# Paired strips of a two-layer decoder: the fourth block summed in the third sum's bank, and the down strips' block sums made of turned tiles

## The chip, the cores and the metric

The kernel runs on one core of one Trainium2 chip. The metric is the time of one execution on the device in microseconds (us); the time before is the median of three runs. A profile is one further execution, taken with the hardware profiler. Its engines are PE (TensorE, matmul), PEld (its weight loads), DVE (VectorE), ACT (ScalarE), POOL (GpSimd) and SP (SyncE, which here only issues DMAs).

## The reference

Two layers of a decoder work on x, 256 rows of 2048 in fp32. Each layer has a mixer (window attention and a gated linear recurrence, side by side, joined by a matrix `w_out`), a gated FFN of width 5632 and a gated addition of per-layer inputs (called ple below):

```
h = rms_norm(x, pre_mix_gain[i])
m = concat([attention, recurrence]) @ w_out[i]
x = x + rms_norm(m, post_mix_gain[i])
h = rms_norm(x, pre_ffn_gain[i])
f = (silu(h @ w_ffn_gate[i]) * (h @ w_ffn_up[i])) @ w_ffn_down[i]
x = x + rms_norm(f, post_ffn_gain[i])
gate = sigmoid(rms_norm(x, ple_gain[i]) @ w_ple_gate[i])
x = x + (p[i] @ w_ple_proj[i]) * gate
```

## The kernel before

**Products.** Every matrix product is made in three matmuls, since each fp32 operand is kept as a high and a low part: high by high, low by high, high by low. Weights come in pieces of 256 x 512 (`wr`, 128 partitions x 1024), fetched by SP's queue. ACT makes the high part by a cast (`wh`, L305), DVE the low part by a subtraction (`wl`, L315). There are ten buffers of `wr` and seven each of `wh` and `wl`, so a cast can run only some pieces ahead of PE. Activations stand turned, with the contraction on the partitions, as high and low parts in tiles `ck`. An output strip is 512 columns wide and has two row halves (t = 0, 1) of 128 rows, each with a bank of PSUM; matmuls have the shape 128 x 128 times 128 x 512. There are two pools of PSUM banks, four banks each: "acc" (`psum(...)`) and "ms" (`bank()`). Temporary tiles of 128 x 512 come from the pool `nat`, twelve buffers.

**A pair of strips.** `paired` (L399) makes two strips at once from the same left side: wa's strip with the banks e (`acce`, half 0) and a (`acca`, half 1), and wb's with c (`accc`) and d (`accd`). For two contraction pieces of 256 (three with `half`), it needs seven block products in place of eight: sums of blocks of the left side (`mixed` L360, `mixed_half`) and differences of weight blocks (`sub`, L434 on DVE) are multiplied, and the results are added. `fast()` does that part. A bank u of the pool "ms" runs through three sums: the first is copied by ACT (`saved`, L427) to x[0]; `second()` goes on in the same bank and copies it to y[0]; `third()` goes on again and copies it to x[1]. p5, the copy of a first sum in c, gets u added on DVE (L496) and becomes y[1]. All other pieces follow in `plain`, a loop over pieces that feeds two banks. d is a fresh bank, taken after all this, with the plain products alone. At the end `done_a` and `done_b` take a bank and the saved sum that belongs to it, and add them on DVE (`summed`, L395, or the down strips' `done`, L1229).

`paired` runs 20 times in each layer: twice for `w_out`; ten times for a gate strip with its up strip (`gated`, n = 1 to 10); seven times for the down strips; once for the ple gate (`after` given).

**Groups of the FFN.** Hidden strips come in groups of 2, 3, 3 and 3 (`FF_GROUPS`). `gated(n)` makes hidden strip n: gate by silu on ACT (L1184), times up on DVE (L1191), a transpose in 32 x 32 blocks on DVE (L251), a store and a fetch by DMA that put the blocks in their places (`shuffled`; the fetched tile is called d there), and then, some ticks later (`later`; a tick is a step of the loop over pieces), a split into a high part by ACT (L203) and a low part by DVE (L204): the `ck` tiles of that strip. When a group is complete, its four down strips follow: strips 0 and 1 as a pair, then 2 and 3 as a pair (in the last group these two go singly). The block sums for these pairs are made by `mixed(first)`, eight ticks after the last gated strip starts, of the `ck` tiles of the group's first hidden strip: two full adds of high and low (L367), four sums of quarters (L373), and two splits. In groups of three, the first down pair has `mixed_order`: the plain products of both strips but the last two pieces, with `second` inside, and then the last two pieces, since the group's last hidden strip is just being split. (The build takes group 0 with three gated strips, 0 to 2, ahead of its down strips of 0 and 1.)

**Order.** The code gives a program order. The framework's scheduler lays the instructions of each engine into a queue at build time, moving products between the places where the data permit it; each engine runs its queue in order, and waits are semaphores. The names with numbers in the rows of the order are tiles (`wl_6236`), and a bank of "ms" is `ms_...`, whichever of u or others it holds.

Of the kernel before, what the change touches and what calls it, by code (L numbers as in the profile page):

```python
# [9 lines left out]
F32R = mybir.dt.float32r  # L10
# [5 lines left out]
P = 128  # L16
# [31 lines left out]
def decoder(ctx: ExitStack, tc: tile.TileContext, x, p, positions, w_in, attn_sinks,  # L48
# [328 lines left out]

    def mixed_half(x):
# [20 lines left out]
    def paired(lhs, sums, wa, wb, cols, done_a, done_b, nch=8, row0=0, skews=(0, 0),  # L399
               after=None, mixed_order=False, half=None):  # L400
# [41 lines left out]
        def fast():  # L442
            mix = sums()
            r11, r12 = fetch_w(wa, base, cols[0]), fetch_w(wb, base, cols[1])
            if half:
                more = half()
                g, p = fetch_w(wa, base + 2, cols[0]), fetch_w(wb, base + 2, cols[1])
            r21, r22 = fetch_w(wa, base + 1, cols[0]), fetch_w(wb, base + 1, cols[1])
            u = bank()
            acc(u, block(0, 0), parts(r11))  # L450
            if half:
                gx = parts(g)
                acc(u, block(2, 0), gx, (0,))
# [10 lines left out]
            acc(e, block(1, 0), parts(r21))  # L464
            if half:
                acc(e, block(2, 0), gx, (1,))
# [3 lines left out]
            acc(a, block(1, 1), parts(r21))  # L470
            if half:
# [3 lines left out]
                acc(a, block(2, 1), g24, (1,))  # L475
# [11 lines left out]
            def third():  # L487
# [8 lines left out]
                V.tensor_tensor(p5, u, p5, op=ALU.add)  # L496
                y.append(p5)
                tick()
            return e, a, c, x, y, second, third

        head = 3 if half else 2

        def plain(w, col, banks, skew, end, c0=head, c1=nch, then=None):
            n = c1 - c0
            ws = {}
            for i in range(n + skew):
                if i < n:
                    ws[i] = load_w(w, base + c0 + i, col)
                    acc(banks[0], block(c0 + i, 0), ws[i])
                    if i == n - 1 and end:  # L510
                        end(0)
                if i >= skew:
                    acc(banks[1], block(c0 + i - skew, 1), ws[i - skew])
# [6 lines left out]
        e, a, c, x1, x2, second, third = fast()  # L520
# [23 lines left out]
        d = psum("accd")  # L544
# [205 lines left out]
    for l in range(DEPTH):  # L750
# [427 lines left out]
        def gated(n, last, first):  # L1178
            col = n * W
            gate = {}  # L1180

# [8 lines left out]
            def done_up(t, ps):  # L1190
                V.scalar_tensor_tensor(gate[t], ps, rx2(t)[:, 0:1], gate[t],  # L1191
                                       op0=ALU.mult, op1=ALU.mult)
                d = shuffled(gate[t], slow=False)
                later(wait, lambda: split_shuffled(d, None, hl, t))

# [7 lines left out]
            if last:  # L1203
# [131 lines left out]
```

## Time and profile before

| | |
|---|---|
| median of three runs | 2377.96 us |
| lowest, highest | 2377.86, 2381.11 us |
| the profiled execution | 2380.66 us |
| its span | 2378.9 us |
| granted TensorE clock, mean | 0.998 |
| HBM read, written | 474.57 MB, 29.36 MB |

A row of a group reads: line, engine, operation, output <- inputs, shape, count | busy us, mean ns of one | idle time of the engine just before them and what ended most of it. A row of the timeline reads: start, duration, engine, line, operation, count and, in brackets, the idle time before it with what ended it. A row of the waits: who waited for what, us in total, times, longest. A row of the windows: from:to, length, busy time (and count) of PE, PEld, DVE, ACT and POOL, then PE's granted clock, DMA's share and GB/s. A matmul's own duration (0.39) is longer than its distance to the next, since they are pipelined.

### The profile page before, as it was taken

Reading aid. Unit: us, or ns where it says so; the run is one execution under the profiler, and the core shown is the slowest. Engines: PE = TensorE matmul, PEld = TensorE weight load, DVE = VectorE, ACT = ScalarE, POOL = GpSimd, SP = SyncE. Lnnn points to the kernel's source line nnn. Section 1 sums busy time; section 2 is a strip of 40 time slices with the busy share of each in tenths; the row PEclk is TensorE's granted clock in tenths of the full one; section 3 lists DMA queues with packets and bytes.
Section 4 is the critical chain, followed back from the end, with each engine's and each line's share of the span. In section 5 each row is a group of like instructions: output and inputs, shape, how many; then the busy total and the mean of one; then the engine's idle time right before and its main releaser. Section 6 shows DMA issues by size and latency. Waiting matters only on the chain.

```text
span 2378.9 us, 31721 instructions
## 1 busy us (share of the span) xinstructions
PE 2358.3 (99%) x10951; PEld 1950.6 (82%) x10951; DVE 2026.5 (85%) x2703; ACT 1398.0 (59%) x2000; POOL 106.6 (4%) x213
## 2 busy tenths in 40 slices
PE   9999999999999999999999999999999999999999
PEld 7888887887888888888788888878878888888887
DVE  7687987999999899888777879779999989998885
ACT  6565466556556555657556554665566565565564
POOL 3100001000000000001010000010000000000010
PEclk9999999999999999999999999999999999999999
DMA  8666467657566664766776663675765575667753
GB/s 290 216 187 203 151 199 250 223 199 244 181 226 219 241 230 166 272 220 203 227 222 207 184 209 132 226 257 180 241 219 193 206 254 198 230 209 251 243 169 133
DMA packets 301666, 506.05 MB, mean 213 GB/s; under 512 B 23712, under 2 KB 69696, under 8 KB 301504
## 3 DMA queue, kind: packets, MB, share of 16 engines
q1 hardware_dynamic: 301200, 503.93, 63.6%
q8 instruction: 86, 1.41, 0.2%
q14 instruction: 76, 0.62, 0.1%
q10 hardware_dynamic: 240, 0.07, 0.0%
q0 software_dynamic: 64, 0.02, 0.0%
HBM read 474.57 MB, written 29.36 MB: 212 GB/s over the span
## 4 chain that ended last, share of the span: by engine, by line
PE 92%; DVE 4%; issue 1%; DMA 1%; ACT 1%; POOL 1%; SPq 0%; DVEq 0%; ACTq 0%; POOLq 0%
PE acc L331 9%; PE acc L330 9%; PE acc L333 9%; PE accc L418 5%; PE accc L421 5%; PE accc L422 5%; PE acca L422 4%; PE acce L422 4%; PE acce L418 4%; PE acca L418 4%; PE acca L421 4%; PE acce L421 4%; PE accd L422 3%; PE accd L418 3%; PE accd L421 3%; PE ms L418 3%
## 5 line engine op out<-in xcount | busy, mean ns | idle before, releaser
L305 ACT CAST wh<-wr 128x1024 fp32r<-128x1024 f32 x980 | 1006.0, 1051 | 722.9 <-DVE wr L434 209.3
L315 DVE TENSOR_TENSOR wl<-wr,wh 128x1024 fp32r<-128x1024 f32 x980 | 1163.0, 1217 | 212.7 <-ACT wh L305 204.9
L330 PE MATMUL acc<-wh,ck 128*128 128x512 f32 x1056 | 417.5, 396 | 0.8 <-ACT ck L203 0.8
L331 PE MATMUL acc<-wh,ck 128*128 128x512 f32 x1056 | 413.4, 392 | 0.0
L333 PE MATMUL acc<-wl,ck 128*128 128x512 f32 x1056 | 412.2, 391 | 0.8 <-DVE wl L315 0.8
L434 DVE TENSOR_TENSOR wr<-wr 128x1024 f32<-128x1024 f32 (+1 forms) x240 | 243.8, 1038 | 0.8
L333 PEld LDWEIGHTS acc<-wl,ck 128*128 128x128 f32 x1056 | 198.7, 188 | 43.0 <-DVE wl L315 1.7
L331 PEld LDWEIGHTS acc<-wh,ck 128*128 128x128 f32 x1056 | 198.9, 188 | 40.3 <-DVE ck L204 0.4
L330 PEld LDWEIGHTS acc<-wh,ck 128*128 128x128 f32 x1056 | 198.5, 188 | 40.6 <-ACT ck L203 1.0
L418 PE MATMUL acca<-wh,ck 128*128 128x512 f32 x468 | 182.6, 390 | 3.1 <-ACT wh L305 3.1
L422 PE MATMUL acca<-wl,ck 128*128 128x512 f32 x468 | 182.3, 390 | 1.1 <-DVE wl L315 1.1
L418 PE MATMUL acce<-wh,ck 128*128 128x512 f32 x468 | 182.7, 390 | 0.4 <-ACT wh L305 0.4
L422 PE MATMUL acce<-wl,ck 128*128 128x512 f32 x468 | 182.3, 390 | 0.3 <-DVE wl L315 0.2
L421 PE MATMUL acce<-wh,ck 128*128 128x512 f32 x468 | 182.1, 389 | 0.0
L421 PE MATMUL acca<-wh,ck 128*128 128x512 f32 x468 | 182.1, 389 | 0.0
L422 PE MATMUL accd<-wl,ck 128*128 128x512 f32 x368 | 144.7, 393 | 0.0
L418 PE MATMUL accd<-wh,ck 128*128 128x512 f32 x368 | 143.7, 390 | 0.0
L421 PE MATMUL accd<-wh,ck 128*128 128x512 f32 x368 | 143.2, 389 | 0.0
L421 PE MATMUL accc<-wh,ck 128*128 128x512 f32 x368 | 143.2, 389 | 0.0
L422 PE MATMUL accc<-wl,ck 128*128 128x512 f32 x368 | 143.2, 389 | 0.0
L418 PE MATMUL accc<-wh,ck 128*128 128x512 f32 x368 | 143.1, 389 | 0.0
L418 PEld LDWEIGHTS acca<-wh,ck 128*128 128x128 f32 x468 | 87.8, 188 | 22.9 <-ACT wh L305 4.8
(277 smaller groups left out, 3362.2 us busy)
## 6 DMA issues: line engine op xcount, KB each, us to landing
wr<-in_w_in_dram SPq DMA_DIRECT2D x176, 512.0 KB, 4.9
wr<-in_w_ffn_gate_dram SPq DMA_DIRECT2D x176, 512.0 KB, 6.0
wr<-in_w_ffn_up_dram SPq DMA_DIRECT2D x176, 512.0 KB, 6.1
wr<-in_w_ffn_down_dram SPq DMA_DIRECT2D x176, 512.0 KB, 7.4
wr<-in_w_out_dram SPq DMA_DIRECT2D x64, 512.0 KB, 4.9
wr<-in_w_ple_gate_dram SPq DMA_DIRECT2D x64, 512.0 KB, 5.5
turn<-nat SPq DMA_DIRECT2D x86, 256.0 KB, 2.6
nat<-turn SPq DMA_DIRECT2D x344, 64.0 KB, 3.6
```

Source lines behind the costliest of these rows:

```text
L305: marks["hi"] = S.copy(hi, raw)
L315: marks["lo"] = V.tensor_tensor(lo, raw, hi.bitcast(F32), op=ALU.subtract)
L330: T.matmul(ps[t], xh, hi[:, k], start=first, stop=False)
L331: T.matmul(ps[t], xl, hi[:, k], start=False, stop=False)
L333: marks[t, c] = marks["pe"] = T.matmul(ps[t], xh, lo[:, k], start=False, stop=last)
L418: T.matmul(ps, xh, hi[:, k], start=id(ps) not in opened, stop=False, skip_group_check=True)
L421: T.matmul(ps, xl, hi[:, k], start=False, stop=False, skip_group_check=True)
L422: marks["pe"] = T.matmul(ps, xh, lo[:, k], start=False, stop=k == ks[-1], skip_group_check=True)
L434: V.tensor_tensor(dst, p, q, op=ALU.subtract)
```

## The change

Two things are changed.

First, the bank d is no longer a fresh one: u, once `third()` has copied it to x[1], simply takes the plain products of the fourth block on top of its sum. So the add of u to p5 (L496) is gone, and `done_b(1)` adds the bank and p5 as they are. In `paired` with `after` (ple), u is taken from the pool "acc" as `accu`; elsewhere it stays in "ms", now until the end of the pair. In the rows of the order the fourth block's products are therefore those on u's `ms_...`.

Second, the down strips' block sums are made by `mixed_turned`, of the two fetched tiles d of the group's second hidden strip (both row halves), before they are split, and no longer of the `ck` tiles of the first. The two full adds (L367) fall away there, the four sums of quarters are made on other views. It runs two ticks after that strip's split was set for. The pair's sums then stand for the second hidden strip (`q=2`: pieces 2 and 3), so these weight pieces are fetched first, and the plain products run over pieces 0, 1, 4, 5 (`rest`).

```diff
+    def mixed_turned(d):
+        out = [[nat((P, 2, 2, P), F32R) for i in range(2)] for _ in range(2)]
+        a = [[x[0][:, 2 * c:2 * c + 2] for x in d] for c in range(2)]
+        s = [nat((P, 2, 2, P)) for _ in range(2)]
+        s1, s2, s3, s4 = (quarters(s[i][:, j]) for i in range(2) for j in range(2))
+        for dst, p, q, op in ((s1, a[0][1], a[1][1], ALU.add), (s2, s1, a[0][0], ALU.subtract),
+                              (s3, a[0][0], a[0][1], ALU.subtract), (s4, a[1][0], s2, ALU.subtract)):
+            V.tensor_tensor(dst, p, q, op=op)
+        for i in range(2):
+            split(s[i], out[0][i], out[1][i])
+        return lambda i: lambda k: tuple(a[(i - 1) // 2][:, (i - 1) % 2, k] for a in out)
...
-            u = bank()
-            acc(u, block(0, 0), parts(r11))
+            u = psum("accu") if after else bank()
+            acc(u, block(q, 0), parts(r11))
...
                 x.append(saved(u))
-                V.tensor_tensor(p5, u, p5, op=ALU.add)
                 y.append(p5)
...
-        e, a, c, x1, x2, second, third = fast()
+        e, a, c, d, x1, x2, second, third = fast()
...
-            plain(wa, cols[0], (e, a), 0, None, c1=nch - 2, then=second)
+            plain(wa, cols[0], (e, a), 0, None, cs=rest[:-2], then=second)
             third()
-            d = psum("accd")
-            plain(wb, cols[1], (c, d), 0, None, c1=nch - 2)
-            plain(wa, cols[0], (e, a), 0, end_a, c0=nch - 2)
-            plain(wb, cols[1], (c, d), 0, end_b, c0=nch - 2)
+            plain(wb, cols[1], (c, d), 0, None, cs=rest[:-2])
+            plain(wa, cols[0], (e, a), 0, end_a, cs=rest[-2:])
+            plain(wb, cols[1], (c, d), 0, end_b, cs=rest[-2:])
...
-        d = psum("accd")
         plain(wb, cols[1], (c, d), skews[1], end_b)
...
                 d = shuffled(gate[t], slow=False)
+                turned.append(d)
                 later(wait, lambda: split_shuffled(d, None, hl, t))
+                if quad and t == 1:
+                    later(wait + 2, lambda: hx.append(mixed_turned(turned)))
...
-            if last:
-                later(8, lambda: hx.append(mixed(first)))
...
-                           mixed_order=s == 1 and glen > 2)
+                           mixed_order=s == 1 and glen > 2, q=2)
```

In the changed file the lines stand 9 to 14 further down: L305, L315, L203, L204 and L251 are as before; the products of `acc` are L431, L434 and L435 (before L418, L421, L422), `saved` is L440, `sub` L447, `summed` L408, the up strip's product L1202.

The order on PE, at the mixed-order pair of the second group of layer 0. Before, from the last products of acca on a plain piece (`acca_6126` ends just ahead of these rows) to the first product of the second sum (`ms_6086` is u, `accd_6213` is d):

```order
L418 MATMUL accd_6213<-wh_6216,ck_5354 128x512 [waits Activation_49]
L421 MATMUL accd_6213<-wh_6216,ck_5355 128x512
L418 MATMUL acce_6113<-wh_6252,ck_5705 128x512 [waits Activation_49]
L422 MATMUL accd_6213<-wl_6218,ck_5354 128x512 [waits DVE_49]
L418 MATMUL accd_6213<-wh_6216,ck_5354 128x512
L421 MATMUL accd_6213<-wh_6216,ck_5355 128x512
L422 MATMUL accd_6213<-wl_6218,ck_5354 128x512
L418 MATMUL accd_6213<-wh_6234,ck_5354 128x512
L421 MATMUL accd_6213<-wh_6234,ck_5355 128x512
L421 MATMUL acce_6113<-wh_6252,ck_5706 128x512 [waits DVE_49]
L422 MATMUL accd_6213<-wl_6236,ck_5354 128x512 [waits DVE_49]
L418 MATMUL ms_6086<-wh_6158,nat_5944 128x512 [waits Activation_49]
```

The same place now (`ms_6062` is u):

```order
L431 MATMUL acca_6102<-wh_6150,ck_4623 128x512
L434 MATMUL acca_6102<-wh_6150,ck_4624 128x512
L435 MATMUL acca_6102<-wl_6152,ck_4623 128x512
L431 MATMUL acce_6089<-wh_6226,ck_5687 128x512 [waits Activation_49]
L434 MATMUL acce_6089<-wh_6226,ck_5688 128x512 [waits DVE_49]
L431 MATMUL ms_6062<-wh_6134,nat_5925 128x512 [waits Activation_49]
```

The nine products of d have moved away from between acca and the second sum; the two products of acce on the newly split hidden strip (`ck_5687` its high part by ACT, `ck_5688` its low part by DVE) are left.

DVE at the same place, from a product of gate and up to the low part of that hidden strip (`ck_5706` before, `ck_5688` now). Before:

```order
L1191 SCALAR_TENSOR_TENSOR nat_5903<-nat_5830,ry0_4017,nat_5903 128x512 [waits DVE_49]
L1191 SCALAR_TENSOR_TENSOR nat_5963<-nat_5759,ry1_4070,nat_5963 128x512 [waits DVE_49]
L251 STREAM_TRANSPOSE nat_6052<-nat_5903 128x4x4x32 [waits DVE_49]
L315 TENSOR_TENSOR wl_6129<-wr_6082,wh_6127 128x1024 [waits Activation_49]
L315 TENSOR_TENSOR wl_6144<-wr_6140,wh_6142 128x1024 [waits DMAHW2_49,Activation_49]
L315 TENSOR_TENSOR wl_6160<-wr_6078,wh_6158 128x1024 [waits Activation_49]
L251 STREAM_TRANSPOSE nat_6069<-nat_5963 128x4x4x32 [waits DVE_49]
L315 TENSOR_TENSOR wl_6176<-wr_6172,wh_6174 128x1024 [waits DMAHW3_49,Activation_49]
L315 TENSOR_TENSOR wl_6192<-wr_6084,wh_6190 128x1024 [waits PE_49,Activation_49]
L315 TENSOR_TENSOR wl_6202<-wr_6080,wh_6200 128x1024 [waits PE_49,Activation_49]
L315 TENSOR_TENSOR wl_6218<-wr_6214,wh_6216 128x1024 [waits DMAHW4_49,PE_49,Activation_49]
L204 TENSOR_TENSOR ck_5706<-nat_6056,ck_5705 128x4x128 [waits DMAHW4_49,DMAHW3_49,DMAHW5_49,DMAHW2_49,Activation_49]
```

Now:

```order
L251 STREAM_TRANSPOSE nat_6028<-nat_5885 128x4x4x32 [waits DVE_49]
L1202 SCALAR_TENSOR_TENSOR nat_5940<-nat_5741,ry1_4066,nat_5940 128x512 [waits DVE_49]
L315 TENSOR_TENSOR wl_6120<-wr_6116,wh_6118 128x1024 [waits DMAHW2_49,Activation_49]
L315 TENSOR_TENSOR wl_6136<-wr_6054,wh_6134 128x1024 [waits Activation_49]
L315 TENSOR_TENSOR wl_6152<-wr_6148,wh_6150 128x1024 [waits DMAHW3_49,Activation_49]
L251 STREAM_TRANSPOSE nat_6045<-nat_5940 128x4x4x32 [waits DVE_49]
L315 TENSOR_TENSOR wl_6168<-wr_6060,wh_6166 128x1024 [waits PE_49,Activation_49]
L315 TENSOR_TENSOR wl_6178<-wr_6056,wh_6176 128x1024 [waits PE_49,Activation_49]
L315 TENSOR_TENSOR wl_6192<-wr_6188,wh_6190 128x1024 [waits DMAHW4_49,PE_49,Activation_49]
L315 TENSOR_TENSOR wl_6210<-wr_6206,wh_6208 128x1024 [waits DMAHW5_49,PE_49,Activation_49]
L315 TENSOR_TENSOR wl_6228<-wr_6224,wh_6226 128x1024 [waits DMAHW6_49,PE_49,Activation_49]
L204 TENSOR_TENSOR ck_5688<-nat_6032,ck_5687 128x4x128 [waits DMAHW5_49,DMAHW4_49,DMAHW6_49,DMAHW3_49,Activation_49]
```

Ahead of these rows stand, before, the two adds of L395; now the add of accc, one wl, the first product of gate and up, and the other add. From the add of accc to the low part there are thus seven wl before and nine now, and the rest is the same. On ACT the two instructions ahead of the second sum have changed places: the cast of one more weight piece (`wh_6244`) now stands ahead of the cast of `ck_5687`.

PE at the first down pair of group 0, which has no mixed order. Before (`accd_5141` is d, `ms_5190` the next pair's u, `ms_5012` this pair's u):

```order
L418 MATMUL accd_5141<-wh_5144,ck_4274 128x512 [waits Activation_49]
L421 MATMUL accd_5141<-wh_5144,ck_4275 128x512
L418 MATMUL ms_5190<-wh_5191,ck_3826 128x512 [waits Activation_49]
L422 MATMUL accd_5141<-wl_5146,ck_4274 128x512 [waits DVE_49]
L418 MATMUL accd_5141<-wh_5144,ck_4274 128x512
L421 MATMUL accd_5141<-wh_5144,ck_4275 128x512
L422 MATMUL accd_5141<-wl_5146,ck_4274 128x512
L418 MATMUL accd_5141<-wh_5162,ck_4274 128x512
L421 MATMUL accd_5141<-wh_5162,ck_4275 128x512
L421 MATMUL ms_5190<-wh_5191,ck_3827 128x512
L422 MATMUL accd_5141<-wl_5164,ck_4274 128x512 [waits DVE_49]
L418 MATMUL ms_5012<-wh_5084,nat_4868 128x512 [waits Activation_49]
```

Now (`ms_5176` is the next pair's u, `ms_5000` this pair's):

```order
L435 MATMUL acca_5040<-wl_5090,ck_3822 128x512
L431 MATMUL ms_5176<-wh_5177,ck_4270 128x512 [waits Activation_49]
L434 MATMUL ms_5176<-wh_5177,ck_4271 128x512
L435 MATMUL ms_5176<-wl_5179,ck_4270 128x512 [waits DVE_49]
L431 MATMUL ms_5000<-wh_5072,nat_4861 128x512 [waits Activation_49]
```

The nine products of d are gone from here too; three of the next pair's first sum stand ahead of the second sum, one more than before, the third on a low part (`wl_5179`) that DVE makes after two other pieces and a split.

More of the change, by code (lines that the diff above doesn't have):

```diff
@@ L399, in paired @@
     def paired(lhs, sums, wa, wb, cols, done_a, done_b, nch=8, row0=0, skews=(0, 0),
-               after=None, mixed_order=False, half=None):
+               after=None, mixed_order=False, half=None, q=0):
         base = row0 // (2 * P)
@@ L443, in fast @@
             mix = sums()
-            r11, r12 = fetch_w(wa, base, cols[0]), fetch_w(wb, base, cols[1])
+            r11, r12 = fetch_w(wa, base + q, cols[0]), fetch_w(wb, base + q, cols[1])
             if half:
                 more = half()
-                g, p = fetch_w(wa, base + 2, cols[0]), fetch_w(wb, base + 2, cols[1])
-            r21, r22 = fetch_w(wa, base + 1, cols[0]), fetch_w(wb, base + 1, cols[1])
-            u = bank()
-            acc(u, block(0, 0), parts(r11))
+                g, p = fetch_w(wa, base + q + 2, cols[0]), fetch_w(wb, base + q + 2, cols[1])
+            r21, r22 = fetch_w(wa, base + q + 1, cols[0]), fetch_w(wb, base + q + 1, cols[1])
+            u = psum("accu") if after else bank()
+            acc(u, block(q, 0), parts(r11))
             if half:
                 gx = parts(g)
-                acc(u, block(2, 0), gx, (0,))
+                acc(u, block(q + 2, 0), gx, (0,))
             x = [saved(u)]
@@ L463, in fast @@
             e = psum("acce")
-            acc(e, block(1, 0), parts(r21))
+            acc(e, block(q + 1, 0), parts(r21))
             if half:
-                acc(e, block(2, 0), gx, (1,))
+                acc(e, block(q + 2, 0), gx, (1,))
             sub(r11, r22, r11)
@@ L469, in fast @@
             a = psum("acca")
-            acc(a, block(1, 1), parts(r21))
+            acc(a, block(q + 1, 1), parts(r21))
             if half:
@@ L474, in fast @@
                 g24 = parts(g)
-                acc(a, block(2, 1), g24, (1,))
+                acc(a, block(q + 2, 1), g24, (1,))
                 sub(p[:, 0], p[:, 1], p[:, 0])
@@ L495, in third, with plain @@
                 x.append(saved(u))
-                V.tensor_tensor(p5, u, p5, op=ALU.add)
                 y.append(p5)
                 tick()
[L499 to L504, printed above, removed]
+            return e, a, c, u, x, y, second, third
+        rest = [i for i in range(nch) if not q <= i < q + (3 if half else 2)]
+        def plain(w, col, banks, skew, end, cs=rest, then=None):
+            n = len(cs)
             ws = {}
@@ L507, in plain @@
                 if i < n:
-                    ws[i] = load_w(w, base + c0 + i, col)
-                    acc(banks[0], block(c0 + i, 0), ws[i])
+                    ws[i] = load_w(w, base + cs[i], col)
+                    acc(banks[0], block(cs[i], 0), ws[i])
                     if i == n - 1 and end:
@@ L512, in plain @@
                 if i >= skew:
-                    acc(banks[1], block(c0 + i - skew, 1), ws[i - skew])
+                    acc(banks[1], block(cs[i - skew], 1), ws[i - skew])
                 if then and i == 0:
@@ L1176, in decoder, with gated @@
         sx = []
-        def gated(n, last, first):
+        def gated(n, last, quad):
             col = n * W
             gate = {}
+            turned = []
             def done_gate(t, ps):
@@ L1213, in decoder @@
                 n = len(hidden)
-                gated(n, n == want - 1, hidden[ff0] if n > ff0 else None)
+                gated(n, n == want - 1, n == want - 2)
             hid = hidden[ff0:ff0 + glen]
```

## The prediction

> **What bounds the kernel now.** I read the page's first part, then the groups by line, the waits of PE, and then the timeline at the places where the order of instructions changes. First the busy times:
>
> ```profile
> PE 2358.3 (99%) x10951; PEld 1950.6 (82%) x10951; DVE 2026.5 (85%) x2703; ACT 1398.0 (59%) x2000; POOL 106.6 (4%) x213
> ```
>
> PE is busy for 2358.3 of 2378.9 us, so there are about 20 us in which it does nothing, and the change leaves its number of products alone. What the change can win is therefore some of those 20 us; what it can lose has no such limit. The groups that the change removes, whole or in part, are DVE's:
>
> ```profile
> L496 DVE TENSOR_TENSOR nat<-ms,nat 128x512 f32<-128x512 f32 x40 | 27.4, 684 | 3.7 <-ACT nat L427 3.7
> L367 DVE TENSOR_TENSOR nat<-ck 128x512 f32<-128x512 f32 x28 | 18.7, 681 | 0.0
> ```
>
> and the waits of PE that could go with them are few:
>
> ```profile
> PE acca L418 <- ACT wh L305: 3.1, 4, 1.3
> PE ms L418 <- ACT nat L427: 2.2, 1, 2.2
> ```
>
> So the question is at each pair of strips: which product is next on PE's queue, and is its operand there?
>
> **Part 1, DVE's work.** 40 adds of L496 go (27.4 us), and 16 of the 28 of L367 (16 x 0.681 = 10.9 us): the eight groups of down strips lose two each. DVE falls from 2026.5 to about 1988 us, 84% of the span. DVE as a whole bounds nothing at 85%, so of these 38 us I count only what shows at a named place. The four quarter sums stay, the turned tiles live two ticks longer, and the weight pieces come in another order but in the same number on SP's queue; nothing in PE's list of waits names a tile of nat or a fetch at a down pair, so I take 0, at most 1 us in all if one add (0.68) is late once or twice.
>
> **Part 2, the fourth block waits for a copy.** The fourth block's first product now writes the bank that ACT has just to copy. In a gated pair:
>
> ```profile
> 467.08 0.58 ACT L427 COPY nat<-ms 128x512 f32<-128x512 f32 x1
> ...
> 468.14 0.39 PE L418 MATMUL accd<-wh,ck 128*128 128x512 f32 x1
> ```
>
> The copy ends at 467.08 + 0.58 = 467.66, 0.48 before the product that must now wait for it, behind six products of accc that stay between. So at the 20 gated pairs the wait is hidden; without that cover it would cost up to 6 x 0.227 = 1.4 each. At the first pair of w_out the copy is later:
>
> ```profile
> 332.09 0.58 ACT L427 COPY nat<-ms 128x512 f32<-128x512 f32 x1
> ...
> 332.47 0.39 PE L418 MATMUL accd<-wh,ck 128*128 128x512 f32 x1
> ```
>
> 332.67 is 0.20 too late for 332.47, but one or two more products stand in between in the new order (0.23 each): 0.05, at most 0.25, at two places: **+0.1**.
>
> **Part 3, the fillers ahead of the second sum.** This is the largest term. Before, the fourth block had a bank of its own, and nine of its products stood between the last product of acca and the second sum (the first rows of the order, in the section on the change). They cannot stand there any more: the bank's three sums must be made and copied first. At the mixed-order pairs only two products of acce are left in between, and the second of these needs the low part of the turned hidden strip (ck, L204) from DVE. PE before, from the end of accc of the strip ahead to the second sum:
>
> ```profile
> 648.16 0.39 PE L422 MATMUL accc<-wl,ck 128*128 128x512 f32 x1
> ...
> 660.40 0.39 PE L422 MATMUL acca<-wl,ck 128*128 128x512 f32 x1
> 660.63 0.39 PE L418 MATMUL accd<-wh,ck 128*128 128x512 f32 x1
> ...
> 662.78 0.40 PE L421 MATMUL acce<-wh,ck 128*128 128x512 f32 x1
> ...
> 663.35 0.39 PE L418 MATMUL ms<-wh,nat 128*128 128x512 f32 x1
> ```
>
> One product starts 0.227 after another when nothing is waited for (660.40 to 660.63). DVE in the same time:
>
> ```profile
> 649.48 0.68 DVE L395 TENSOR_TENSOR nat<-accc,nat 128x512 f32<-128x512 f32 x1
> 650.08 0.68 DVE L395 TENSOR_TENSOR nat<-accd,nat 128x512 f32<-128x512 f32 x1
> 650.68 1.41 DVE L1191 SCALAR_TENSOR_TENSOR nat<-nat,ry 128x512 f32<-128x512 f32 x2
> 652.00 0.70 DVE L251 STREAM_TRANSPOSE nat<-nat 128x512 f32<-128x512 f32 x1
> 652.63 3.46 DVE L315 TENSOR_TENSOR wl<-wr,wh 128x1024 fp32r<-128x1024 f32 x3
> 656.00 0.70 DVE L251 STREAM_TRANSPOSE nat<-nat 128x512 f32<-128x512 f32 x1
> 656.63 4.59 DVE L315 TENSOR_TENSOR wl<-wr,wh 128x1024 fp32r<-128x1024 f32 x4
> 661.13 0.68 DVE L204 TENSOR_TENSOR ck<-nat,ck 128x512 fp32r<-128x512 f32 x1
> ```
>
> There is no idle time in this stretch: from the add of accc to the end of L204 at 661.81, DVE does two adds, two L1191, two transposes, seven wl and the split. In the new order it does the same and two more wl (nine), each 1.14 apart ((656.00 - 652.63)/3 = 1.12, (661.13 - 656.63)/4 = 1.13, so 2.27 for two). The add of accc can't start before accc's last product has ended, 648.16 + 0.39 = 648.55, some 648.60 with the signal: a head start of 0.88. The three adds that go just ahead of this stretch (two of L367, one of L496, about 2.0 us) are enough for that, so I take it whole. The split then ends at 661.81 + 2.27 - 0.88 = 663.20, and at 664.08 without a head start. Product 2 of acce starts at 663.25, and the second sum 0.23 after that, 663.48, where PE with nothing to wait for would be at 660.40 + 3 x 0.227 = 661.08. Lost 2.40. The old rows lost 663.35 - (660.40 + 12 x 0.227 = 663.12) = 0.23 by small waits. Net 2.17 at each of six places (two further groups in this layer, three in the next): **+13.0**. The bound from below: were DVE in time, ACT would still be late:
>
> ```profile
> 659.10 0.62 ACT L203 CAST ck<-nat 128x512 fp32r<-128x512 f32 x1 [0.16 <-DMA nat<-turn]
> 660.60 1.06 ACT L305 CAST wh<-wr 128x1024 fp32r<-128x1024 f32 x1 [0.89 <-PE acca L421]
> 661.56 0.58 ACT L427 COPY nat<-ms 128x512 f32<-128x512 f32 x1
> ```
>
> On ACT the cast of a weight piece that waits for PE until 660.60 now stands ahead of the cast of ck: 661.56, then 0.62 to 662.18, product 1 at 662.23 where it stood free at 660.63. 1.6 less 0.23 is 1.4 each, 8.2 in all. From above: 3.05 each (no head start), 18.3. The order shows these rows at six places; their times I read at this one.
>
> **Part 4, group 0.** Its first down pair has no mixed order. The new order puts three products of the next pair's first sum between acca and the second sum, and the third needs a wl:
>
> ```profile
> 532.52 0.39 PE L422 MATMUL acca<-wl,ck 128*128 128x512 f32 x1
> ...
> 535.45 0.39 PE L418 MATMUL ms<-wh,nat 128*128 128x512 f32 x1
> ...
> 546.36 0.39 PE L422 MATMUL acce<-wl,ck 128*128 128x512 f32 x1
> 548.04 0.50 PE L418 MATMUL acca<-wh,ck 128*128 128x512 f32 x1 [1.30 <-ACT wh L305]
> 548.38 0.40 PE L421 MATMUL acca<-wh,ck 128*128 128x512 f32 x1
> 549.00 0.50 PE L418 MATMUL acce<-wh,ck 128*128 128x512 f32 x1 [0.22 <-ACT wh L305]
> ```
>
> ```profile
> 533.85 2.35 DVE L315 TENSOR_TENSOR wl<-wr,wh 128x1024 fp32r<-128x1024 f32 x2
> ```
>
> Up to that wl DVE does the same set of instructions as before up to the end of this row, 536.20, less a head start taken as in part 3: 535.32, and the product 0.05 later. It would be due at 532.52 + 3 x 0.227 = 533.20, so 2.17 lost; the old rows lost 535.45 - 532.52 - 12 x 0.227 = 0.2. Against that the waits at 546.36 go, since DVE's four subtractions for the next weights now stand ahead of the last adds and L496 is gone: (1.68 - 0.23) + (0.62 - 0.23) and two starts of 0.11 = 2.06. Net -0.1 at two places: **-0.2** (from -4.1, if wl is in time, to +1.6 without the head start). The end of group 0's second pair:
>
> ```profile
> 570.88 0.39 PE L422 MATMUL acce<-wl,ck 128*128 128x512 f32 x1
> 571.52 0.50 PE L418 MATMUL acca<-wh,ck 128*128 128x512 f32 x1 [0.25 <-ACT wh L305]
> 571.85 0.40 PE L421 MATMUL acca<-wh,ck 128*128 128x512 f32 x1
> 572.78 0.50 PE L422 MATMUL acca<-wl,ck 128*128 128x512 f32 x1 [0.53 <-DVE wl L315]
> 573.11 0.40 PE L418 MATMUL acca<-wh,ck 128*128 128x512 f32 x1
> ```
>
> 0.41 + 0.10 + 0.70 + 0.10 = 1.3 are lost here; with L496 out of that queue they go, at two places: **-2.6** (or 0).
>
> **Part 5, the ple pair of layer 0, and the clock.** A wait for a copy, and then a slow clock:
>
> ```profile
> 1156.07 0.80 PE L418 MATMUL ms<-wh,sum 128*128 128x512 f32 x1 [2.25 <-ACT nat L427]
> ```
>
> ```profile
> 1153.80:1156.00 2.20, 0.03 (x1) 0.00 (x0) 1.99 (x3) 2.12 (x5) 0.37 (x1) 1.00 0.87 316
> 1156.00:1159.40 3.40, 3.33 (x8) 2.65 (x9) 1.41 (x2) 2.24 (x4) 0.23 (x1) 0.50 0.74 197
> ```
>
> After 2.2 us of idle PE the granted clock was 0.50 for 3.40 us: eight products, 3.40/8 = 0.43 apart, 8 x (0.43 - 0.227) = 1.6 us. The 1.45 and 0.39 at 546.36 had no such sequel (the next product follows 0.34 later). The sum's bank moves to the other pool here and the stall is cut in two, so I count half of the 1.6: **-0.8** (from -4.0, all of it gone, to +0.8).
>
> The sum so far is 0.1 + 13.0 - 0.2 - 2.6 - 0.8 = **+9.5**. Parts 3 and 4 make eight new stalls of 2.2 to 2.4 us, about the 2.2 that brought the half clock, though in part 3 they fall into two pieces with a product between. I take half of them to be followed by it: 4 x 1.6 = **+6.4** (0 to 12.8). The profiled execution, 2378.9 + 1.76 = 2380.66, would become 2396.6; the median lies 2.70 below the profiled one, so 2377.96 + 15.9 = **2393.9**.
>
> The Trainium skill, page "TensorE: Matmul & The Clock Gate", section "What's actually happening", has the clock fall to half after at least one idle window of about 3.4 us, in windows that run free of the program. By that rule no stall of 2.4 us would cost more than itself, and the sum would stay at +9.5 (rival 1); the trace speaks against its threshold with 2.2 us of idle ahead of a clock of 0.50, and for its window with the length of that stretch, 3.40.
>
> **The rivals.**
> 1. No half clock: no stall is long enough, or it is broken too early. For it: the stalls of part 3 are broken by a product, and 1.45 + 0.39 had no sequel. Against it: 2.2 us at 1153.80. 2377.96 + 9.5 = 2387.5. Chance 0.25.
> 2. Half clock after all eight: 9.5 + 12.8 = 22.3, 2400.3. For it: the ple pair's 2.2 is no longer than theirs. Against it: the two pieces. Chance 0.17.
> 3. Faster. The lighter DVE has the split of ck (L204) ready by 661.0, the two wl behind which it stands being made earlier, so the second sum is not late; then the two stalls of group 0 go, 2 x 2.06 = 4.1, and 2.6, and the ple pair's 4.0: -10.7, 2367.3. It decides at 661.0: with L204 done by then there is no loss. For it: 38 us less on DVE. Against it: DVE is without a gap from 649.48 to 661.81, and of the removed adds none lies in that stretch. Chance 0.08.
> 4. No change: the stalls of part 3 stay at ACT's bound, 8.2 in all, no clock is lost, and group 0 gives back its 2.6 and, with wl in time, 4.1: 8.2 + 0.1 - 4.1 - 2.6 - 0.8 = +0.8, 2378.8. For it: in part 4 only one wl stands between. Against it: DVE's chain, as for rival 3. Chance 0.10.
>
> **How the numbers follow.** The forecast itself (half of the stalls with a slow clock) has the remaining 0.40 (with up to seven or as few as one of the eight). What a measurement of this kernel can tell from no change is about 0.2%, 4.8 us. The low end is part 3 at ACT's bound (8.2) without a slow clock, 9.5 - 4.8 = 4.7, taken down to 4: 2382; the high end is 18.3 in part 3 and six of eight slow clocks, 9.5 + 5.3 + 9.6 = 24.4, or 13.0 and all eight with the ple pair at its +0.8, 23.9: 2403. That leaves out rivals 3 and 4 and a few in a hundred above. Faster 0.08, same 0.10, slower 0.82.
>
> **What would show it.** In the profile of the changed kernel: PE idle for about 1.6 and then 0.8 us on acce ahead of the second sum at each of the six mixed-order pairs, released by ACT's ck and by DVE's L204; a wait for a wl of about 2.2 in front of the first pair's second sum in group 0; none at the ends of group 0's pairs; granted clock 0.50 in some of the stretches behind. DVE near 1988 us. It would be wrong if the timeline shows L204 of ck done before PE's last acca product, or the second sum running on without a gap, or if the fourth block's first product waited at the gated pairs (20 of them: 0.3 each would be 6 us).

## The result

The changed kernel takes 2397.0 us (median of 4 runs, 2393.93 to 2399.29) against 2378.28 us before (4 runs, 2377.86 to 2381.11): a ratio of 1.0076, 95% interval 1.0063 to 1.0088. It is slower by 18.7 us, where 15.9 were forecast. The profiled execution took 2398.53 us with a span of 2396.7, 17.8 longer than before; the rows below are of it.

The busy times of the changed kernel, and the first rows of what PE waited for:

```profile
PE 2365.4 (99%) x10951; PEld 1955.7 (82%) x10951; DVE 1997.5 (83%) x2647; ACT 1401.3 (58%) x2000; POOL 104.3 (4%) x213
```

```profile
PE acce L431 <- ACT ck L203: 8.6, 6, 1.4
PE ms L435 <- DVE wl L315: 4.0, 2, 2.0
PE acce L434 <- DVE ck L204: 3.3, 6, 0.5
```

None of these rows was there before, and their counts are the places of the forecast: six mixed-order pairs, twice each, and group 0's first pair in both layers. The rows `acca <- wh` (3.1 us) and `ms <- nat` (2.2 us) of before are gone, and so is every wait at the ends of group 0's pairs. DVE has 56 instructions less and 29.0 us less to do.

The mixed-order pair of the second group, on PE:

```profile
658.94 0.39 PE L435 MATMUL acca<-wl,ck 128*128 128x512 f32 x1
660.76 0.50 PE L431 MATMUL acce<-wh,ck 128*128 128x512 f32 x1 [1.43 <-ACT ck L203]
661.81 0.51 PE L434 MATMUL acce<-wh,ck 128*128 128x512 f32 x1 [0.55 <-DVE ck L204]
662.15 0.40 PE L431 MATMUL ms<-wh,nat 128*128 128x512 f32 x1
```

With nothing to wait for, the fourth row would start at 658.94 + 3 x 0.227 = 659.62. It starts at 662.15: 2.53 lost, in two pieces of 1.59 and 0.82 and a slower start behind them (0.12). On ACT, the weight cast that waits for PE, which stood ahead of the copy of u before too, has come ahead of the cast of ck as well:

```profile
659.14 1.04 ACT L305 CAST wh<-wr 128x1024 fp32r<-128x1024 f32 x1 [1.66 <-PE acca L434]
660.10 0.61 ACT L203 CAST ck<-nat 128x512 fp32r<-128x512 f32 x1
660.62 0.58 ACT L440 COPY nat<-ms 128x512 f32<-128x512 f32 x1
```

and on DVE, from the add of accc to the low part of ck:

```profile
647.13 0.69 DVE L408 TENSOR_TENSOR nat<-accc,nat 128x512 f32<-128x512 f32 x1 [1.11 <-PE accc L435]
647.74 1.22 DVE L315 TENSOR_TENSOR wl<-wr,wh 128x1024 fp32r<-128x1024 f32 x1
...
655.42 5.73 DVE L315 TENSOR_TENSOR wl<-wr,wh 128x1024 fp32r<-128x1024 f32 x5
661.06 0.70 DVE L204 TENSOR_TENSOR ck<-nat,ck 128x512 fp32r<-128x512 f32 x1
```

The add now waits 1.11 for accc's last product, so the head start is used up whole; then DVE runs without a gap to 661.76, and PE's product starts 0.05 later, at 661.81. Group 0's first pair:

```profile
532.54 0.39 PE L435 MATMUL acca<-wl,ck 128*128 128x512 f32 x1
532.76 0.39 PE L431 MATMUL ms<-wh,ck 128*128 128x512 f32 x1
532.99 0.39 PE L434 MATMUL ms<-wh,ck 128*128 128x512 f32 x1
535.40 0.50 PE L435 MATMUL ms<-wl,ck 128*128 128x512 f32 x1 [2.02 <-DVE wl L315]
535.74 0.39 PE L431 MATMUL ms<-wh,nat 128*128 128x512 f32 x1
```

The third product of the next pair's first sum waits 535.40 - 532.99 - 0.23 = 2.18 for its low part. Then the clock. The windows behind two of the six stalls, the one above and that of the next group (columns as in the prediction):

```profile
662.00:665.40 3.40, 3.40 (x15) 2.66 (x15) 1.70 (x2) 1.90 (x3) 0.00 (x0) 1.00 0.95 255
...
852.00:855.40 3.40, 3.40 (x9) 2.65 (x9) 0.74 (x1) 0.78 (x1) 0.00 (x0) 0.55 1.01 260
```

The same stall of 2.5 us left the granted clock at 1.00 at the first place, and was followed by half the clock at the second: 9 products in 3.40 us and not 15. In this execution five of the eight stalls (four of the six, one of the two in group 0) have such a stretch behind them; what decides which is in the last section.

### The profile page after: what moved, and what is told of

It reads as the page before. It is cut to its first block, busy times and chain, and to the rows that moved or that the text cites. A ratio compares the mean times of both kernels' runs of the same rounds, so it can differ in the third digit from the quotient of the medians.

```text
span 2396.7 us, 31644 instructions
## 1 busy us (share of the span) xinstructions
PE 2365.4 (99%) x10951; PEld 1955.7 (82%) x10951; DVE 1997.5 (83%) x2647; ACT 1401.3 (58%) x2000; POOL 104.3 (4%) x213
## 5 line engine op out<-in xcount | busy, mean ns | idle before, releaser
L305 ACT CAST wh<-wr 128x1024 fp32r<-128x1024 f32 x980 | 1012.1, 1052 | 794.9 <-DVE wr L447 215.4
L315 DVE TENSOR_TENSOR wl<-wr,wh 128x1024 fp32r<-128x1024 f32 x980 | 1169.2, 1220 | 252.8 <-ACT wh L305 233.7
L447 DVE TENSOR_TENSOR wr<-wr 128x1024 f32<-128x1024 f32 (+1 forms) x240 | 243.4, 1042 | 1.2
L431 PE MATMUL acce<-wh,ck 128*128 128x512 f32 x468 | 183.1, 391 | 8.6 <-ACT ck L203 8.6
L434 PE MATMUL acce<-wh,ck 128*128 128x512 f32 x468 | 183.6, 392 | 3.3 <-DVE ck L204 3.3
L431 PE MATMUL acca<-wh,ck 128*128 128x512 f32 x468 | 182.2, 389 | 0.6 <-ACT nat L1285 0.6
L435 PE MATMUL acce<-wl,ck 128*128 128x512 f32 x468 | 182.2, 389 | 0.0
L435 PE MATMUL acca<-wl,ck 128*128 128x512 f32 x468 | 182.1, 389 | 0.0
L434 PE MATMUL acca<-wh,ck 128*128 128x512 f32 x468 | 182.1, 389 | 0.0
L435 PE MATMUL ms<-wl,ck 128*128 128x512 f32 x440 | 171.5, 390 | 4.0 <-DVE wl L315 4.0
L431 PE MATMUL ms<-wh,ck 128*128 128x512 f32 x440 | 172.5, 392 | 0.0
L434 PE MATMUL ms<-wh,ck 128*128 128x512 f32 x440 | 171.3, 389 | 0.0
L434 PE MATMUL accc<-wh,ck 128*128 128x512 f32 x368 | 143.2, 389 | 0.0
L435 PE MATMUL accc<-wl,ck 128*128 128x512 f32 x368 | 143.2, 389 | 0.0
L431 PE MATMUL accc<-wh,ck 128*128 128x512 f32 x368 | 143.2, 389 | 0.0
L431 PEld LDWEIGHTS acce<-wh,ck 128*128 128x128 f32 x468 | 87.8, 188 | 28.8 <-ACT ck L203 11.1
```

What stands on the lines that cost most here:

```text
L305: marks["hi"] = S.copy(hi, raw)
L315: marks["lo"] = V.tensor_tensor(lo, raw, hi.bitcast(F32), op=ALU.subtract)
L431: T.matmul(ps, xh, hi[:, k], start=id(ps) not in opened, stop=False, skip_group_check=True)
L434: T.matmul(ps, xl, hi[:, k], start=False, stop=False, skip_group_check=True)
L435: marks["pe"] = T.matmul(ps, xh, lo[:, k], start=False, stop=k == ks[-1], skip_group_check=True)
L447: V.tensor_tensor(dst, p, q, op=ALU.subtract)
```

## Experiments

Each kernel was timed in turn with the kernel before, in three sessions on three chips; the kernel before had medians of 2379.10, 2379.24 and 2378.98 us in them (21 to 25 runs each).

### The two parts, each alone

`e1_sums_only`: a fresh bank d and the add of u again in the changed kernel. The same edit, with another condition, serves two later kernels.

```diff
-            u = psum("accu") if after else bank()
+            own = True
+            u = psum("accu") if after and not own else bank()
...
                 x.append(saved(u))
+                if own:
+                    V.tensor_tensor(p5, u, p5, op=ALU.add)
                 y.append(p5)
...
-            return e, a, c, u, x, y, second, third
+            return e, a, c, None if own else u, x, y, second, third
...
+        d = d or psum("accd")
```

> The second part alone: sums made of the turned tiles, but a fresh bank for the fourth block and the add of u to p5, as before. Theory (the shared bank takes nine filler products away from in front of the second sum): the fillers are back, so no wait of 1.6 and 0.8 on acce at the six mixed-order pairs and none of 2.2 in group 0; no half clock from them; time 2374 to 2380. Rival (the turned sums, with their later tiles and other order of pieces, make the waits): waits of 2.4 at the six pairs stay, 2391 to 2399.

Measured: 2374.63 us (10 runs, 2373.79 to 2378.01), ratio to before 0.9986 (0.9976 to 0.9996). The six waits and the two are gone, as the theory had it, and the second part alone is a gain of some 4 us, at the edge of what can be told. Part of it is the ple pair, whose wait is 1.71 here where it was 2.41 before, with no half clock behind it.

`e2_bank_only`: the old sums in the changed kernel.

```diff
-                if quad and t == 1:
-                    later(wait + 2, lambda: hx.append(mixed_turned(turned)))
...
+            if last:
+                later(8, lambda: hx.append(mixed(first)))
...
-                           mixed_order=s == 1 and glen > 2, q=2)
+                           mixed_order=s == 1 and glen > 2)
```

> The first part alone: the fourth block goes on in u's bank, the down strips' sums are made of the first strip's ck tiles as before (two full adds more at each of eight groups, 10.9 us of DVE). Theory: waits of about 2.4 at six pairs and of about 2.2 at two, half clock behind about half of them, 2393 to 2401. Rival (the turned sums make the waits): no such waits, 2374 to 2380.

Measured: 2382.38 us (10 runs, 2381.54 to 2384.93), ratio 1.0017 (1.0007 to 1.0026). Neither theory: there are waits, but small ones (at the six places, and two of 1.2 at group 0's pairs in each layer), no half clock behind them, and the time is 11 us below the theory's range. The fillers are missing here as well, and PE's order at the six places is the same. The rows of PE and then of ACT:

```profile
659.56 0.39 PE L435 MATMUL acca<-wl,ck 128*128 128x512 f32 x1
659.78 0.39 PE L431 MATMUL acce<-wh,ck 128*128 128x512 f32 x1
660.27 0.51 PE L434 MATMUL acce<-wh,ck 128*128 128x512 f32 x1
661.34 0.50 PE L431 MATMUL ms<-wh,nat 128*128 128x512 f32 x1 [0.56 <-ACT nat L440]
```

```profile
658.00 0.61 ACT L203 CAST ck<-nat 128x512 fp32r<-128x512 f32 x1
659.76 1.05 ACT L305 CAST wh<-wr 128x1024 fp32r<-128x1024 f32 x1 [1.15 <-PE acca L434]
660.71 0.58 ACT L440 COPY nat<-ms 128x512 f32<-128x512 f32 x1
```

ck's cast stands ahead of the weight cast that waits for PE, and on DVE seven wl stand between the add of accc and ck's low part, not nine, so PE's second product starts at 660.27 with 0.26 lost. What is left is the copy of u, behind the weight cast: 661.34 - 659.56 - 3 x 0.227 = 1.10 at each of the six places. So the missing fillers open the gap, but the other 1.4 of the 2.53 us come of where the split of ck stands on DVE's and ACT's queues, and that is what the second part has moved. The parts do not add: +3.3 and -4.5 alone, +18.7 together.

### A fresh bank in the six pairs alone

`e3_own_in_mixed`: as `e1_sums_only`, with `own = mixed_order`.

> The changed kernel, but the six mixed-order pairs take a fresh bank for the fourth block and add u to p5. Theory: the six waits of 2.41 go (14.5 us, with the four half clocks of 1.6 behind them 20.9); the two of 2.2 in group 0 and one half clock stay; 2397 - 20 = 2377, between 2374 and 2381. Rival (the whole of the shared bank counts, the gated pairs with it): only part of that, 2384 or more.

Measured: 2375.04 us (10 runs, 2373.04 to 2376.93), ratio 0.9984 (0.9975 to 0.9993). The order there now has twelve products of d ahead of the second sum, and the trace has no gap in front of it:

```profile
661.80 0.39 PE L435 MATMUL accd<-wl,ck 128*128 128x512 f32 x1
662.02 0.39 PE L431 MATMUL acce<-wh,ck 128*128 128x512 f32 x1
662.25 0.39 PE L431 MATMUL ms<-wh,nat 128*128 128x512 f32 x1
```

Six pairs of forty make the 22 us between this kernel and the changed one (their stalls and half clocks are 6 x 2.53 + 4 x 1.6 = 21.6 in the changed kernel's profile); the other thirty-four bear the shared bank without cost, apart from group 0's 2.2, which stay. With them it is no slower than `e1_sums_only`.

### The half clock by itself

`e4_idle`: products of the unit matrix in the gap.

```diff
+                if then and i == 1 and mixed_order:
+                    with behind("pe"):
+                        spare = psum("spare")
+                        for _ in range(12):
+                            T.matmul(spare[:, 0:P], ident, ident, start=True, stop=True)
```

> The changed kernel with twelve products of the unit matrix (128 x 128 x 128) put on PE's queue behind the last product of acca at the six mixed-order pairs, into a spare bank; their results are not used. They fill most of the wait of 1.59 and leave the one of 0.82. Theory (the clock falls to half after about 2 us of idle PE): the waits end when they did, and the half clock behind the six pairs goes: 4 x 1.64 = 6.6 less, 2388 to 2393. Rival (the half clock comes of the stall in another way, or of the DMA load at that time): it stays, 2394 to 2400.

Measured: 2393.67 us (4 runs, 2393.01 to 2394.37). Each of the twelve stands as two records in the trace, 0.11 apart, so they took 2.6 us, enough for both pieces of the wait, not the first alone:

```profile
659.63 0.40 PE L435 MATMUL acca<-wl,ck 128*128 128x512 f32 x1
659.87 2.84 PE L532 MATMUL spare<-ident 128*128 128x128 f32 x24
662.47 0.48 PE L431 MATMUL acce<-wh,ck 128*128 128x512 f32 x1
662.78 0.39 PE L431 MATMUL ms<-wh,nat 128*128 128x512 f32 x1
```

The order has changed with them: the second product of acce now stands behind the second sum. The sum therefore starts 662.78 - 659.63 - 2 x 0.227 = 2.70 late, where 2.53 were lost before. What holds it is no longer a wait: ACT's copy of u ends at 661.88, and the last of the twelve starts at 662.43. PE is busy all the time, and the windows of 3.40 us behind all six places have a granted clock of 1.00, this one among them:

```profile
851.90:855.30 3.40, 3.40 (x21) 2.92 (x20) 1.77 (x3) 1.65 (x3) 0.00 (x0) 1.00 0.95 268
```

So the half clock comes of the idle time of PE. It is worth 4 x 1.6 = 6.4 us at the six places of the changed kernel's profile. The time fell by 3.3 only, but here both stalls of group 0 had one behind them, not one of two, so that three are saved, 4.8 us; the 0.17 at each of the six places takes 1.0 of that back, and one stall of group 0 is 0.3 longer.

### Which wait ends last

`e8_split_late`: the split of the last hidden strip ordered behind the copy of c. (`behind` orders an instruction after a marked one.)

```diff
-            S.copy(b, ps)
+            marks["saved"] = S.copy(b, ps)
...
-                later(wait, lambda: split_shuffled(d, None, hl, t))
+                def split_it():
+                    with behind("saved") if last else nullcontext():
+                        split_shuffled(d, None, hl, t)
+                later(wait, split_it)
```

> The changed kernel, with the split of a group's last hidden strip ordered behind the copy of the first sum in c. The two products of acce that need it then stand behind the second sum, which comes right after acca. Theory: DVE's low part no longer counts (0.82 at six pairs gone), but the second sum waits for the copy of u, which stands on ACT's queue behind the same weight cast: a wait of about 1.6 at six pairs stays, too short alone for the half clock; 2397 - 4.9 - 4 x 1.6 = 2385.5, between 2383 and 2392. Rival (the wait for the split strip is all there is): all six waits go, 2374 to 2379.

Measured: 2384.05 us (9 runs, 2383.13 to 2386.34). The wait for ck is gone, and the one behind it shows:

```profile
659.50 0.39 PE L435 MATMUL acca<-wl,ck 128*128 128x512 f32 x1
661.28 0.50 PE L431 MATMUL ms<-wh,nat 128*128 128x512 f32 x1 [1.39 <-ACT nat L440]
```

661.28 - 659.50 - 0.23 = 1.55 at each of six places, the copy of u behind the same weight cast (which starts at 659.70, when PE frees its buffer). No half clock follows any of them.

`e10_ck_cast`: the cast of ck and the weight cast exchanged on ACT. On DVE the low part of ck has then come ahead of one wl, and on PE a third product of acce, which needs that wl, ahead of the second sum.

```diff
-            split(d, h, lo)
+            marks["ck", t] = split(d, h, lo)[0]
...
-                    ws[i] = load_w(w, base + cs[i], col)
+                    raw = fetch_w(w, base + cs[i], col)
+                    with behind(("ck", 0)) if wait and i else nullcontext():
+                        ws[i] = load_w(None, 0, 0, raw=raw)
...
-            plain(wa, cols[0], (e, a), 0, end_a, cs=rest[-2:])
+            plain(wa, cols[0], (e, a), 0, end_a, cs=rest[-2:], wait=True)
```

> The changed kernel with one pair of instructions exchanged on ACT's queue at the six mixed-order pairs: the cast of the split (ck) stands ahead of the last weight cast again, as in the kernel before. On DVE the low part of ck then stands ahead of one wl, but a third product of acce, which needs that wl, has come in front of the second sum. Theory (the last of DVE's chain decides, ACT only the first piece): the wait falls into two pieces of about 1.2 and 1.1, the second sum starts no earlier than 0.2 before; 2392 to 2398. Rival (the exchanged cast on ACT is the cause): the waits fall to 0.8 as in the kernel with the shared bank alone, 2380 to 2386.

Measured: 2393.90 us (4 runs, 2393.23 to 2395.07). At five of the six places the first product of acce is free (at the other it waits 0.76), and the two behind it wait for DVE:

```profile
849.00 0.39 PE L431 MATMUL acce<-wh,ck 128*128 128x512 f32 x1
850.50 0.49 PE L434 MATMUL acce<-wh,ck 128*128 128x512 f32 x1 [1.11 <-DVE ck L204]
851.64 0.55 PE L435 MATMUL acce<-wl,ck 128*128 128x512 f32 x1 [0.64 <-DVE wl L315]
```

850.50 - 849.00 - 0.23 = 1.27 and 851.64 - 850.50 - 0.23 = 0.91, and with the slower start behind them 2.3 at each place. So ACT's exchanged cast made the first piece of the stall, but DVE's chain decides its end.

### The order mended

`e9b_copy_first`: the split behind the copy of c, and the casts of the pair's last two wa pieces behind it too, so that they can no longer block ACT's queue.

```diff
-            p5 = saved(c)
+            p5 = nat()
+            marks["p5"] = S.copy(p5, c)
...
-                    ws[i] = load_w(w, base + cs[i], col)
+                    raw = fetch_w(w, base + cs[i], col)
+                    with behind("p5") if wait else nullcontext():
+                        ws[i] = load_w(None, 0, 0, raw=raw)
...
-            plain(wa, cols[0], (e, a), 0, end_a, cs=rest[-2:])
+            plain(wa, cols[0], (e, a), 0, end_a, cs=rest[-2:], wait=True)
...
-                later(wait, lambda: split_shuffled(d, None, hl, t))
+                def split_it():
+                    with behind("p5") if last else nullcontext():
+                        split_shuffled(d, None, hl, t)
+                later(wait, split_it)
```

> As the kernel with the split ordered late, and the weight casts of the last two pieces ordered behind the copies of u and c on ACT's queue at the six mixed-order pairs. Theory: copies are done before acca's last product, the second sum runs on without a gap, and the six waits go with their half clocks: 2397 - 14.5 - 6.6 = 2376, between 2373 and 2380. Rival (with the fillers gone something else comes late, a cast or a low part behind the copies): waits of 1 us or more at other places, 2382 or more.

Measured: 2371.73 us (7 runs, 2371.07 to 2372.24), ratio to before 0.9972 (0.9961 to 0.9983). ACT copies u at 653.38, where it did so at 660.62 in the changed kernel:

```profile
653.38 0.58 ACT L440 COPY nat<-ms 128x512 f32<-128x512 f32 x1
653.86 0.59 ACT L475 COPY nat<-accc 128x512 f32<-128x512 f32 x1
658.45 0.62 ACT L203 CAST ck<-nat 128x512 fp32r<-128x512 f32 x1 [4.00 <-DMA nat<-turn]
```

and the second sum follows acca without a gap:

```profile
657.66 0.39 PE L435 MATMUL acca<-wl,ck 128*128 128x512 f32 x1
657.89 0.39 PE L431 MATMUL ms<-wh,nat 128*128 128x512 f32 x1
```

No fillers are needed when the copy is early. This is the fastest kernel of the study, faster than before and than the change. Group 0's wait has become 1.58, and no stretch of half clock is left behind any stall.

`e13_own_copy_first`: the same order with a fresh bank in all pairs (`own = True`).

> As e9b_copy_first, but with a fresh bank for the fourth block and the add of u to p5 in all pairs. If the shared bank is itself worth something once the order is mended (DVE's 27 us, the waits at group 0's pairs): slower than e9b_copy_first by 1.5 to 4, 2373 to 2376. Rival (the order is everything, the bank nothing): 2370 to 2372.5.

Measured: 2375.41 us (11 runs, 2373.33 to 2376.86), ratio 0.9982 (0.9973 to 0.9991). That is 3.7 above `e9b_copy_first` (each median from its own session) and about that of `e1_sums_only`, 2374.63: with a fresh bank the order did not matter, and with the shared bank it decides. The sign is surer than the size: all seven runs of `e9b_copy_first` lie below all eleven of this kernel, but the two profiled executions are only 1.8 apart (2372.24 and 2374.05). Its waits at group 0's ends are there as before (`acca <- wh`, 2.0 us; `acca <- wl`, 1.1). So the shared bank is a gain once the copies are early; in the changed kernel the stalls covered it.

### Two tries at group 0

`e9c_copy_first_all` adds to `e9b_copy_first` that each pair's first weight cast goes behind the pair before's copy of c; `e11_u_later` leaves the cast and orders only the products.

```diff
-            acc(u, block(q, 0), parts(r11))
+            with behind("p5") if "p5" in marks else nullcontext():
+                w11 = parts(r11)
+            acc(u, block(q, 0), w11)
```

> As the last, and the first weight cast of each pair is ordered behind the pair before's copy of c, so that in group 0 too the second sum stands ahead of the next pair's products. Theory: the two waits of 2.2 and their half clock go as well, while the waits that the change took away at group 0's pairs (3.3 each layer) and at the ple pair stay away: 2369 to 2375, under the kernel before. Rival: the waits at group 0's ends come back, 2375 to 2380.

```diff
-            acc(u, block(q, 0), parts(r11))
+            w11 = parts(r11)
+            with behind("second") if q and cols[0] else nullcontext():
+                acc(u, block(q, 0), w11)
...
+                marks["second"] = marks["pe"]
                 y.append(saved(u))
```

> As e9b_copy_first, and in group 0 the products of the second down pair's first sum are ordered behind the first pair's second sum, on PE alone; its weight cast is not delayed. Theory (the waits of 1.58 in group 0 are only a product placed too early): they go, and nothing comes later in their place: 2371.7 - 3.2 = 2368.5, between 2367 and 2371. Rival (as in e9c_copy_first_all, what is put later is missed at the pair's end): 2371 to 2376.

Measured: 2376.54 us (10 runs, 2375.42 to 2380.23) and 2374.75 us (11 runs, 2372.78 to 2376.92), both slower than `e9b_copy_first`; the theory failed in both. In the first, PE at the pair's end:

```profile
545.37 0.39 PE L435 MATMUL acce<-wl,ck 128*128 128x512 f32 x1
548.08 0.50 PE L431 MATMUL acca<-wh,ck 128*128 128x512 f32 x1 [2.31 <-ACT wh L305]
```

In the second, the third sum waits for the copy of the second, which stands on ACT behind a weight cast that waits for DVE's subtraction:

```profile
535.32 0.39 PE L435 MATMUL accc<-wl,nat 128*128 128x512 f32 x1
537.76 0.50 PE L431 MATMUL ms<-wh,nat 128*128 128x512 f32 x1 [2.05 <-ACT nat L440]
```

```profile
536.17 1.05 ACT L305 CAST wh<-wr 128x1024 fp32r<-128x1024 f32 x1 [3.55 <-DVE wr L447]
537.13 0.58 ACT L440 COPY nat<-ms 128x512 f32<-128x512 f32 x1
```

In both cases the 1.58 came back as 2.2 to 2.5 one step later. What order would lose nothing in group 0 is open.

## Why the prediction held, step by step

- **Part 1.** DVE fell by 29.0 us, not 38: the removed adds are gone to the number (56 instructions), but the rest took longer, L315 alone 1169.2 us where it had 1163.0. As forecast, DVE's sum decided nothing.
- **Part 2, the copy of the third sum.** Hidden, as forecast: PE's list has no wait of a fourth block's product for a copy. At the gated pair of the prediction the copy ends at 467.68 and the product starts at 468.16.
- **Part 3.** Forecast 2.40 lost at each place in pieces of 1.6 and 0.8, measured 1.59 and 0.82; with the slower start behind them, which the sum left out here, 2.53, less the 0.22 of before 2.31, so 13.9 for six (forecast 13.0). The chain of DVE was right to 0.02: all times here are 658.94 - 660.40 = 1.46 earlier than before, and the forecast end of the split, 663.20 - 1.46 = 661.74, was 661.76. What the prediction's heading for this part says, that the lost fillers are the cause, is half of it: `e2_bank_only` lost them and paid 1.10 a place. The two more wl and the exchanged cast, which the sum had counted, were the other half, and they came of the second part of the change. Why the scheduler moved them with the second part is not settled.
- **Part 4.** Forecast 2.17 in front of group 0's second sum, measured 2.18; the waits at the ends of both pairs went as forecast. The sum there was -0.2 and -2.6; measured 2 x (2.29 - 0.21 - 2.06) = 0 and -2.6 (535.74 - 532.54 - 4 x 0.227 = 2.29).
- **Part 5, ple.** Mis-sized. The wait is cut in two, as forecast, and the half clock is gone with it:

```profile
1158.20 0.50 PE L431 MATMUL acca<-wh,ck 128*128 128x512 f32 x1 [0.60 <-ACT nat L1285]
...
1164.64 0.50 PE L431 MATMUL accu<-wh,sum 128*128 128x512 f32 x1 [1.16 <-ACT nat L440]
```

  It cost 2.4 + 1.66 before (wait and slow clock) and costs 0.76 + 1.32 and two slow starts of 0.1 now: -1.8, where -0.8 was forecast. The reason given there, the bank's other pool and the cut in two, is not needed: in `e1_sums_only`, where u stays in "ms", the wait is one piece of 1.71, and no half clock follows it either.
- **The clock.** Four of eight were forecast, five occurred in the profiled execution, 1.6 each: 8.0 for 6.4. The half was a guess: the prediction knew that 2.2 us had once been followed by it, not what decides. By the grid in the last section half is what stalls of this length can expect (an estimate), and the two pieces, which the prediction and its rivals weighed, made no difference where they lay in one stretch of that grid. The four timed runs lie 1.5, 3.1 and 0.8 us apart, with mean granted clocks of 0.997, 0.997, 0.995 and 0.995 from the fastest to the slowest, which fits another number of such stretches in each; only one of them was profiled.
- **The sum.** 0 + 13.9 + 0 - 2.6 - 1.8 + 8.0 = 17.5, and the spans differ by 17.8.

The rivals: "faster" and "no change" fell with the first row of the waits; "no half clock" (2387.5) and "after all eight" (2400.3) fell with the count of five, though the second lies near the slowest run.

## What to carry to other kernels

Before a bank (or buffer) is reused to save an operation, look at what the fresh one allowed: here it fed products into a gap that nobody saw, because it was filled. When an engine's queue is in order, count the instructions ahead of the one that is waited for, on each engine, in the new order, and time them by the rows of the old trace; that gave the stalls to a few hundredths. And if a stall appears, ask which of the waits behind it comes next before removing the first: here the copy stood behind the split, and one cast that waited for PE held up both.

## What was not expected of the hardware

Idle time of PE of 2.2 to 2.5 us at one place, whole or in pieces, was followed by half the granted clock at some places and not at others, with the same instructions: in the profiles of the kernel before, the changed one and the experiments, at 13 places of 25. Of 13 unbroken waits of 1.5 to 1.85 us none was followed by it. Each stretch of half clock is 3.41 us long and costs 1.5 to 1.7.

The traces show what decides it. In the profile of the changed kernel the clock falls at 851.67, 1042.82, 1725.49, 2042.93 and 2234.07 us. These moments are 56, 200, 93 and 56 times 3.4133 us apart, to within 0.01 us: they lie on a grid of fixed spacing, and so do the falls of the other profiles that have more than one. Here are two neighbouring stretches of that grid at the stall that begins at 658.94, and two at the equal stall that begins at 848.80 (the granted clock is the third number from the end):

```profile
657.12:660.53 3.41, 2.21 (x10) 1.50 (x8) 3.41 (x4) 1.75 (x3) 0.00 (x0) 1.00 0.84 287
660.53:663.94 3.41, 2.63 (x10) 1.98 (x11) 2.36 (x3) 1.58 (x4) 0.00 (x0) 1.00 0.94 241
...
848.26:851.67 3.41, 1.44 (x7) 0.62 (x5) 3.41 (x5) 2.54 (x4) 0.00 (x0) 1.00 0.93 294
851.67:855.08 3.41, 3.41 (x8) 2.73 (x9) 1.07 (x1) 0.46 (x1) 0.00 (x0) 0.50 1.01 252
```

The first stall is divided between two stretches, with PE busy for 2.21 and 2.63 us of them, and nothing follows. The second falls into one stretch, with PE busy for 1.44, and the next has half the clock. To compare all places, count PE as idle from 0.227 us behind the start of a product to the start of the next, and leave out the first 30 us of the program, which have other products, and its end. Then, in the twelve profiles, all 13 falls follow a stretch with 2.07 us or more of idle time, and no stretch with 1.95 or less is followed by one. If the border is 2.0 us, stalls like the eight reach it in about half of the possible positions of the grid (an estimate from these figures). Where the border lies in other kernels, no run here shows.

The Trainium skill, page "TensorE: Matmul & The Clock Gate", section "What's actually happening", speaks of an idle window of about 3.4 us, free of the program's start: the window's length and that it runs free agree with the grid, but a window need not be idle as a whole, since 2.07 us of 3.41 were enough here.
